# The state-space loop of a two-layer trunk: its order on four engines, its outer products, its rotation table and its rings of loads

## The chip, the core and the metric

The kernel runs on one core of a Trainium2 chip. The metric is the time of one launch on the device in microseconds, median of the runs shown. Engines: PE (TensorE), DVE (VectorE), ACT (ScalarE), POOL (GpSimd), and SP, which here only issues DMAs.

## The reference

Two residual layers over 512 tokens of width 1024: a state-space mixer (S5), then forgetting attention, each followed by a gated feed-forward block with a short convolution. Every sub-layer is preceded by an RMSNorm whose shift, scale and gate come from a conditioning vector (adaLN). The change touches the first mixer alone:

```
u = h @ w_in
lb = exp(lam * exp(log_dt))                      # complex, 64 groups of 64 states
h[t] = lb * h[t-1] + bb @ u[t]                   # per group: 16 channels drive 64 states
y[t] = Re(c @ h[t]) + d * u[t]
y = gelu(y);  y = y * sigmoid(y @ w_glu);  out = y @ w_out
```

## The kernel before

Everything is fp32. Activations lie as 8 blocks of 128 channels by 512 tokens. A float32 matrix product whose result must be exact is made from rounded parts (`w_hi`, `w_lo`: ACT rounds, DVE takes the rest) as three products; the first mixer's projection and its inner products run in plain fp32.

**The mixer.** Time is cut into B = 64 blocks of L = 8 tokens. Each of the KT = 8 steps m of the loop takes 8 groups (128 channels):

- *projection*: u of block m, eight products of `s5_w_in` with the normalized x (`a_x`, L1196). ACT evicts it (`uf`, L1198), SP writes it to DRAM (`s_ud`, L1201) and reads it back in another layout (`u`, L1203).
- *inputs* (`s5_inputs`): outer products of powers of lambda with B on DVE (`x`, L983, L987); PE multiplies them with `both` (planes of C and of an identity, filled by ACT, L995) into `aux` (L999); ACT evicts `w1` and the convolution kernel `kt` (L1004, L1008). `kt` plus the skip (`dd`, L1009) goes to DRAM (`s_z`) and comes back as a Toeplitz matrix (`tw`, L1016), which ACT masks (`t`, L1021).
- *scan* (`s5_scan`): PE makes the block sums (L1036), DVE rotates them by a table (`s_rot`), so that the recurrence over the 64 blocks becomes real, scans (L1058) and rotates back (`ua`, L1047 to L1068). `cf` are the scan's factors, made by ACT (L1053).
- *outer products out* (`s5_states_out`, `w2`, L963, L972) on DVE, and *outputs* (`s5_outputs`): the Toeplitz part (L1078), then the states' part (L1086), then gelu on ACT (`yg`, L1092) and a way through DRAM (`s_yd`) into `y`, L1096.

Between these, `ada_pe` computes the modulation vectors: each PE pair of products (L212) eats two tiles `raw` of 512 KB from `in_ada_w`. The first two thirds (scale, shift) stand in the startup, the gate and two thirds of the next sub-layer in the loop: twelve pairs, called modulation pairs here. Loads take rooms in rings: `raw` has three, `w_hi` and `w_lo` five each; a load waits until the room's last reader is done. The argument `n` of `raw()` chooses the ring.

**The startup** (up to the first L1196) computes the state-space parameters in small DVE operations of 128x32 (`s5_params`), interleaved with the root of the RMSNorm (`inv_root`, `rs_y`). The scale's columns give `ga` (L174), x is normalized (`a_x`, L1150), and the products of block 0 run between the loads of the shift; the shift is added afterwards by ACT (L1174, L1185) and, for block 0, through a product with the shift column (L1177).

**Order.** The startup stands in a `manual_schedule`: PE, ACT, DVE and SP issue what the program says, in its order. The loop was left to the framework's scheduler, which orders the instructions of all engines by its own cost model and the given priorities; `behind(...)` and `issue_after` only keep some of them from moving ahead. Behind the loop, the first four blocks of the glu product (`glu_head`, L1223) are interleaved the same way: part 0 with the rounded weights `hi`, made by ACT (L1257), part 1 with `lo`.

## Time and profile before

| | us |
|---|---|
| median of 3 runs | 1211.58 (1208.62 to 1212.55) |
| profiled execution, its own time | 1210.89 |
| its span | 1209.1 |
| startup, to the first projection in the loop | 43.0 |
| the loop's first to last block sums (L1036) | 64.7 to 162.9 |
| first product behind the mixer's gate head (L301, mmp) | 198.5 |

A row of a view by windows reads: stretch in us, then for each engine its busy time and the number of its instructions, the clock granted to PE (1.00 is full), the share of the DMA engines and GB/s. A row of a timeline: start, duration of the run of equal instructions, engine, line, operation, out<-in, shape, count, and in brackets the idle time ahead of it with what ended it. One matrix product in fp32 is two PE instructions in the trace. PEld are the weight loads, which overlap PE. SPq rows are the issues of DMAs, and the last number in a row of issues is the median from issue to landing.

### The profile page before, as it was taken

The page shows a single profiled execution, that of the slowest core. Times are in us where ns is not written, and L with a number is a line of the kernel's source. Part 1 is how long each engine was busy: PE and PEld are TensorE (multiplying, and loading weights), DVE is VectorE, ACT ScalarE, POOL GpSimd, SP SyncE. Part 2 cuts the span into 40 slices and gives each one's busy share as a digit, 9 for nine tenths or more (in the row PEclk, how much of TensorE's full clock was granted, in tenths as well). Part 3 has the DMA queues.
Part 4 walks back from the last instruction along what each step waited for, and adds up shares of the span by engine and source line. Part 5 has one row for each costly group of instructions (what it writes and reads, how often), then busy time and mean ns, then how long its engine had stood idle before and what let it go on. Part 6 is the DMA issues. An engine that isn't in the chain of part 4 may idle for free.

```text
span 1209.1 us, 20651 instructions
## 1 busy us (share of the span) xinstructions
PE 1179.1 (98%) x7925; PEld 1015.0 (84%) x7925; DVE 1010.3 (84%) x1900; ACT 612.4 (51%) x1172; POOL 91.1 (8%) x149
## 2 busy tenths in 40 slices
PE   7999999999999999999999999999999999999997
PEld 2566678898989889999899888878989999999987
DVE  7889986879889999998697578876899887888865
ACT  3564554336444455555443566664366555545543
POOL 0000001100000000000000344430000000000000
PEclk9999999999999999999999999999999999999999
DMA  8777787721455545433445543432223432323331
GB/s 334 242 251 247 225 292 272 256 98 36 131 159 172 171 156 165 159 107 97 127 145 193 168 160 126 150 117 94 76 65 102 122 119 82 114 93 110 110 100 70
DMA packets 72849, 181.73 MB, mean 150 GB/s; under 512 B 23103, under 2 KB 25503, under 8 KB 71727
## 3 DMA queue, kind: packets, MB, share of 16 engines
q1 hardware_dynamic: 66127, 156.82, 39.6%
q0 software_dynamic: 6336, 23.07, 5.8%
q8 instruction: 62, 1.02, 0.4%
q10 hardware_dynamic: 288, 0.52, 0.1%
q14 instruction: 36, 0.29, 0.1%
HBM read 173.47 MB, written 6.92 MB: 149 GB/s over the span
## 4 chain that ended last, share of the span: by engine, by line
PE 51%; issue 19%; DVE 17%; DMA 8%; ACT 2%; POOL 1%; SPq 0%; DVEq 0%; POOLq 0%; ACTq 0%
PE mmp L301 23%; PE mmp L570 10%; DVE w_lo L285 5%; PE aux L570 4%; PE mmp L1196 3%; PE mmp L1401 2%; PE aux L1540 2%; DVE conv L622 2%; PE aux L1560 1%; DVE sums L538 1%; DVE nm_t L538 1%; DVE ada_raw L254 1%; DVE h L383 1%; DMA rawd<-in_w_down 1%; PE aux L999 1%
## 5 line engine op out<-in xcount | busy, mean ns | idle before, releaser
L285 DVE TENSOR_TENSOR w_lo<-raw,w_hi 128x1024 fp32r<-128x1024 f32 (+4 forms) x173 | 184.9, 1074 | 25.2 <-ACT w_hi L284 24.7
L284 ACT ACTIVATE w_hi<-raw 128x1024 fp32r<-128x1024 f32 (+4 forms) x173 | 153.9, 899 | 100.6 <-PE mmp L301 47.2
L301 PE MATMUL mmp<-ghi,w_lo 128*128 128x512 f32 (+1 forms) x412 | 147.5, 358 | 1.2 <-DVE w_lo L285 1.2
L301 PE MATMUL mmp<-ghi,w_hi 128*128 128x512 f32 (+1 forms) x412 | 147.8, 359 | 0.3 <-DVE h L383 0.3
L301 PE MATMUL mmp<-glo,w_hi 128*128 128x512 f32 (+1 forms) x412 | 147.3, 358 | 0.0
L301 PE MATMUL mmp<-a_hi,w_hi 128*128 128x512 f32 (+1 forms) x344 | 126.0, 369 | 1.5 <-ACT a_hi L453 1.5
L301 PE MATMUL mmp<-a_hi,w_lo 128*128 128x512 f32 (+1 forms) x344 | 123.7, 360 | 0.0
L301 PE MATMUL mmp<-a_lo,w_hi 128*128 128x512 f32 (+1 forms) x344 | 123.4, 359 | 0.0
L570 PE MATMUL mmp<-w_hi 128*128 128x256 f32 x420 | 116.2, 277 | 1.5 <-DVE nm_t L538 1.3
L570 PE MATMUL mmp<-w_lo,w_hi 128*128 128x256 f32 x420 | 115.9, 276 | 0.0
L570 PE MATMUL mmp<-w_hi,w_lo 128*128 128x256 f32 x420 | 115.7, 276 | 0.0
L577 ACT ACTIVATE nm_h<-mmp 128x256 f32<-128x256 f32 x105 | 39.7, 381 | 108.8 <-PE mmp L570 108.8
L285 DVE TENSOR_TENSOR w_lo<-sums,w_hi 128x1024 fp32r<-128x1024 f32 x78 | 94.8, 1217 | 0.0
L284 ACT ACTIVATE w_hi<-sums 128x1024 fp32r<-128x1024 f32 x78 | 80.9, 1053 | 17.8 <-DVE sums L538 16.1
L301 PEld LDWEIGHTS mmp<-ghi,w_lo 128*128 128x128 f32 x412 | 77.4, 188 | 13.8 <-DVE w_lo L285 2.2
L301 PEld LDWEIGHTS mmp<-ghi,w_hi 128*128 128x128 f32 x412 | 77.4, 188 | 11.0 <-issue 0.5
L301 PEld LDWEIGHTS mmp<-glo,w_hi 128*128 128x128 f32 x412 | 77.4, 188 | 10.2
L570 PEld LDWEIGHTS mmp<-w_hi 128*128 128x128 f32 x420 | 78.8, 188 | 2.1 <-ACT w_hi L284 1.6
L383 DVE SCALAR_TENSOR_TENSOR h<-mmp,par,h 128x512 f32<-128x512 f32 (+1 forms) x104 | 68.6, 663 | 14.1 <-PE mmp L301 13.9
L570 PE MATMUL mmp<-a_hi,w_hi 128*128 128x256 f32 x280 | 78.0, 279 | 2.1 <-ACT nm_h L577 1.9
L570 PEld LDWEIGHTS mmp<-w_lo,w_hi 128*128 128x128 f32 x420 | 78.8, 188 | 0.0
L570 PE MATMUL mmp<-a_hi,w_lo 128*128 128x256 f32 x280 | 77.6, 277 | 1.2 <-DVE w_lo L285 1.2
(320 smaller groups left out, 3086.6 us busy)
## 6 DMA issues: line engine op xcount, KB each, us to landing
raw<-in_w_up SPq DMA_DIRECT2D x88, 512.0 KB, 3.3
raw<-in_ada_w SPq DMA_DIRECT2D x40, 512.0 KB, 5.0
ada_raw<-in_ada_t POOLq DMA_DIRECT2D x40, 512.0 KB, 4.5
nf<-nfd SPq DMA_DIRECT2D x8, 1152.0 KB, 7.1
raw<-in_fox_qk SPq DMA_DIRECT2D x16, 512.0 KB, 3.8
raw<-in_w_down SPq DMA_DIRECT2D x24, 320.0 KB, 2.9
rawd<-in_w_down SPq DMA_DIRECT2D x24, 256.0 KB, 3.3
raw<-in_w_down SPq DMA_DIRECT2D x16, 384.0 KB, 3.4
```

Source lines behind the costliest of these rows:

```text
L254: nc.vector.tensor_tensor_reduce(w, w, self.c_row, 1.0, 0.0, ALU.mult, ALU.add, sums[:, j:j + 1])
L284: self.rounded = nc.scalar.activation(hi, src, AF.Copy).ins
L285: return nc.vector.tensor_tensor(lo, src, hi.bitcast(F32), ALU.subtract)
L301: self.last_mm = self.nc.tensor.matmul(o if len(xt.shape) == 2 else by_place(o), wt, xt, start=(k == 0 and n == 0), stop=(k == nk - 1 and ...
L383: add = self.nc.vector.scalar_tensor_tensor(h, ps, self.par[i][:, 16 + m:17 + m], h, op0=ALU.mult, op1=ALU.add,)
L538: sub = lambda o, u, v, op=ALU.subtract: nc.vector.tensor_tensor(o, u, v, op)
L570: self.last_mm = nc.tensor.matmul(o, wt[:, k], xt[:, k], start=(first and k == 0 and n == 0), stop=(k == H - 1 and n == 2), skip_group_che ...
L577: a = nc.scalar.activation(t, o, AF.Copy)
L622: c = nc.vector.scalar_tensor_tensor(t[:, d:], ps[:, :S - d], cw[:, 2 - d, f:f + 1], t[:, d:], op0=ALU.mult, op1=ALU.add)
L1196: nc.tensor.matmul(ps, w[m][:, k, :], x[:, k], start=(k == 0), stop=(k == KT - 1))
L1401: self.last_mm = nc.tensor.matmul(ps[q, b][:, :n], xt[:, k, tb], wt, start=(k == 0 and i == 0), stop=(k == KT - 1 and i == 2),)
L1540: nc.tensor.transpose(pt[:, r - rs[0], k, :], s[:, r, k * P:(k + 1) * P], self.ident)
```

## The change

The loop and its prologue now stand in a `manual_schedule` too: the order on PE, ACT, DVE and SP is the program's. Within a step: block sums m, gelu of m-1, inputs of m+1, scan m, kernel of m+1, mask m, projection and outer products of m+2, outer products out of m+1, outputs of m, modulation pairs, factors and rotations. The pieces of `s5_inputs` are functions of their own.

The outer products for `w2` become two of 128x1024 instead of four of 128x512 (C lies as three planes side by side, one of them twice). The full rotation table goes: `s_rot` keeps the first 8 blocks, and two tiles `rot` of 8 pairs each are filled from it in turn, with a third plane for minus the sine, so that a rotated sum needs no split. `ada_pe` can load one pair ahead, and its loads and those of `s5_w_in` go round three rings instead of two (`n % 3`). In the startup the turns are interleaved with the parameters' last part, and the root stands behind both; some parameter work moves later.

```diff
             [(t, k) for t in thirds] for k in range(KT)
         ]
         n = 0
-        for step in steps:
+        ws = []
+
+        def load(step):
+            nonlocal n
+            for t, k in step:
+                ws.append(self.raw([P, D], self.io["ada_w"][i, k * P:(k + 1) * P, t * D:(t + 1) * D], n % 3))
+                n += 1
+
+        if ahead:
+            load(steps[0])
+            yield True
+        for s, step in enumerate(steps):
+            if not ahead:
+                load(step)
+            elif s + 1 < len(steps):
+                load(steps[s + 1])
             for j, (t, k) in enumerate(step):
-                w = self.raw([P, D], self.io["ada_w"][i, k * P:(k + 1) * P, t * D:(t + 1) * D], n % 2)
-                n += 1
+                w = ws.pop(0)
                 for q in range(2):
                     qq = 2 * j + q
...
-        y = self.inv_root(stats, NB, log=logs[0])
-        self.s5_turns(pool, co, si, logs[1])
-        in_turn(*logs)
-        yield y
+        self.s5_turns(pool, co, si, logs[0])
+        e = Ew(nc, tp, P, H, "e", ring=ring(0), log=logs[1])
...
-        nc.vector.reciprocal(rd, den)
+        e.do(lambda: nc.vector.reciprocal(rd, den))
         num = e.ts(br, -1.0, ALU.add)
         kr = e.add(e.mul(num, lre), e.mul(bi, lim))
         kr = e.mul(kr, rd, keep("kr"))
         ki = e.sub(e.mul(bi, lre), e.mul(num, lim))
         ki = e.mul(ki, rd, keep("ki"))
-        yield
+        in_turn(*logs)
+        yield self.inv_root(stats, NB)
         w1 = tp.tile([P, L, H], F32, name="s5_w1")
         w2 = tp.tile([P, L, H], F32, name="s5_w2")
 
...
+    def s5_rotations(self, m):
+
+        pairs = slice(m * 4, m * 4 + 8)
+        T = self.s5r.tile([P, 3, 8, B], F32, name="rot", bufs=2)
+        self.nc.scalar.activation(T[:, :2, :, :8], self.rot[:, :, pairs], AF.Copy)
+        self.s5_tables(T[:, :2], pairs, 3, 5)
+        yield
+        self.s5_tables(T[:, :2], pairs, 5, 6)
+        self.nc.scalar.activation(T[:, 2], T[:, 1], AF.Copy, scale=-1.0)
+        yield T
+
+    def s5_outer(self, m, l, b, a, tag):
+
         qs = slice(m * (GM // 2), (m + 1) * (GM // 2))
+        sh = [P, GM // 2, 2 * CG, L]
+        o = self.s5q.tile([P, GM // 2, 2, CG, L], F32, name=tag, bufs=1 if tag == "x" else 2)
+        self.nc.vector.tensor_tensor(
+            o.rearrange("p k r c j -> p k (r c) j"), l[:, qs, None, :].to_broadcast(sh),
+            b[:, qs, a:a + 2, :].rearrange("p k r c -> p k (r c)")[:, :, :, None].to_broadcast(sh), ALU.mult,
+        )
+        return o
+
+    def s5_sums(self, m, l, k, b, a, c, tag):
+
+        t1 = self.s5_outer(m, l, b, a, tag)
+        t2 = self.s5_outer(m, k, b, c, "x2")
         self.nc.vector.tensor_tensor(t1, t1, t2, ALU.add)
         return t1
 
+    def s5_states_out(self, m):
+        return self.s5_sums(m, self.er, self.ei, self.rr, 0, 1, "w2")
+
+    def s5_states_in(self, m):
+        return self.s5_sums(m, self.lr, self.li, self.bb, 1, 0, "x")
...
+    def s5_kernel(self, m, kt, dd):
+
+        nc = self.nc
         nc.vector.tensor_tensor(
             kt.rearrange("p c g -> p (c g)"), kt.rearrange("p c g -> p (c g)"), dd, ALU.add,
         )
+        nc.sync.dma_start(self.z[m][:P], kt.rearrange("p c g -> p (c g)"))
+
+    def s5_toeplitz(self, m):
+
         z = self.z[m]
         R = CG * GM
         tw = self.wpool.tile([P, L, CG, GM], F32, name="tw", tag="w_lo", bufs=WB)
...
+        turns = turns.rearrange("p r g b -> p r (g b)")
+        cb = turns[:, 0:1].to_broadcast([P, 2, W])
         v = ps.rearrange("p r g b -> p r (g b)")
         m1 = pool.tile([P, 2, W], F32, name="m1")
         m2 = pool.tile([P, 2, W], F32, name="m2")
         nc.vector.tensor_tensor(m1, v, cb, ALU.mult)
-        nc.vector.tensor_tensor(m2, v, sb, ALU.mult)
-        nc.vector.tensor_tensor(m1[:, 0], m1[:, 0], m2[:, 1], ALU.add)
-        nc.vector.tensor_tensor(m1[:, 1], m1[:, 1], m2[:, 0], ALU.subtract)
-        cf = pool.tile([P, 2, H4, B], F32, name="cf")
-        for k in range(H4):
-            nc.scalar.activation(
-                cf[:, :, k, :], self.mask[:, None, :].to_broadcast([P, 2, B]), AF.Copy,
-                scale=self.mag8[:, m * H4 + k:m * H4 + k + 1],
-            )
+        nc.vector.tensor_tensor(m2, v[:, ::-1], turns[:, 1:3], ALU.mult)
+        nc.vector.tensor_tensor(m1, m1, m2, ALU.add)
...
-                    w[m] = self.raw([P, KT, P], self.io["s5_w_in"][m], m % 2)
-
-                self.rot = keep.tile([P, 2, G // 2, B], F32, name="s5_rot")
+                    w[m] = self.raw([P, KT, P], self.io["s5_w_in"][m], m % 3)
+
+                self.rot = keep.tile([P, 2, G // 2, 8], F32, name="s5_rot")
...
-            ada = [self.ada_pe(i, (2,), late=True), self.ada_pe(i + 1, (0, 1), late=True)]
-            with self.behind(*behind):
-                for m in range(2):
-                    inputs(m)
-                ws[0] = self.s5_inputs(0)
-            for m in range(KT):
-                if m:
-                    outputs(m - 1)
-                if m > 1:
-                    self.s5_read_y(m - 2)
-                with self.behind(*behind):
-                    if m % 2 == 0:
-                        self.s5_tables(slice(m * 4, m * 4 + 8), 3, 6)
+            ada = itertools.chain(
+                self.ada_pe(i, (2,), late=True, ahead=True), self.ada_pe(i + 1, (0, 1), late=True, ahead=True)
+            )
+            with tc.manual_schedule(engines={ENG.PE, ENG.Activation, ENG.DVE, ENG.SP}):
+                ps = self.aux.tile([KT, P], F32, name="aux")
+                nc.tensor.transpose(ps, self.sc, self.ident)
+                rows = self.tmp.tile([KT, P], F32, name="nm_h", bufs=4)
+                self.s5_signs_c()
+                self.s5_planes_of(0)
+                for k in range(2, 4):
+                    nc.scalar.activation(x[:, k], x[:, k], AF.Identity, bias=self.par[i][:, k:k + 1])
+                load_d(0)
+                load_d(1)
+                load_w(2)
+                next(ada)
+                inputs(0)
+                for k in range(4, KT):
+                    nc.scalar.activation(x[:, k], x[:, k], AF.Identity, bias=self.par[i][:, k:k + 1])
+                read_u(0)
+                turns = self.s5_rotations(0)
+                next(turns)
+                self.s5_kernel(0, kts.pop(0), dds.pop(0))
+                rot = next(turns)
+                x_in[1] = self.s5_states_in(1)
+                w2s[0] = self.s5_states_out(0)
+                tws[0] = self.s5_toeplitz(0)
+                project(1)
+                read_u(1)
+                nc.scalar.activation(rows, ps, AF.Copy)
+                nc.sync.dma_start(self.scd, rows)
+                cfs[0] = self.s5_factors(0)
+                for m in range(KT):
+                    if m + 3 < KT:
+                        load_w(m + 3)
+                    if m + 2 < KT:
+                        load_d(m + 2)
+                    ps = self.s5_blocks(ws[m], us[m])
+                    if m:
+                        self.s5_gelu(m - 1, yps.pop(m - 1))
                     if m + 1 < KT:
-                        ws[m + 1] = self.s5_inputs(m + 1)
+                        self.s5_planes_of(m + 1)
+                        inputs(m + 1)
+                    st = self.s5_scan(rot[:, :, m % 2 * 4:m % 2 * 4 + 4], ps, cfs.pop(m))
+                    if m + 1 < KT:
+                        self.s5_kernel(m + 1, kts.pop(m + 1), dds.pop(m + 1))
+                    t = self.s5_masked(tws.pop(m))
+                    if m:
+                        self.s5_read_y(m - 1)
+                    if m + 1 < KT:
+                        tws[m + 1] = self.s5_toeplitz(m + 1)
                     if m + 2 < KT:
-                        inputs(m + 2)
-                    for _ in range((2, 2, 1, 1, 1, 1, 2, 2)[m]):
-                        next(ada[m >= 2])
-                    if m == 1:
-                        next(ada[0])
+                        project(m + 2)
+                        read_u(m + 2)
+                        x_in[m + 2] = self.s5_states_in(m + 2)
+                    if m == KT - 2:
+                        yhi = self.act.tile([P, KT, S], F32R, name="a_hi")
+                        ylo = self.act.tile([P, KT, S], F32R, name="a_lo")
+                    if m >= KT - 2:
+                        for n in (2 * m - 12, 2 * m - 11):
+                            raw[n] = self.raw([P, KT, P], self.io["s5_w_glu"][n], 2 * (n == HEAD - 1))
+                    if m + 1 < KT:
+                        w2s[m + 1] = self.s5_states_out(m + 1)
+                    yps[m] = self.s5_outputs(us.pop(m), t, w2s.pop(m), st)
+                    ws.pop(m)
+                    for _ in range((2, 2, 2, 2, 2, 1, 2, 1)[m]):
+                        next(ada)
+                    if m + 1 < KT:
+                        cfs[m + 1] = self.s5_factors(m + 1)
+                        if m % 2 == 0:
+                            if m + 2 < KT:
+                                turns = self.s5_rotations(m + 2)
+                                next(turns)
+                        else:
+                            rot = next(turns)
+                    if m == KT - 2:
+                        for k in range(4):
+                            parts(k)
                     if m == KT - 1:
+                        for k in range(4, 6):
+                            parts(k)
                         for n in range(HEAD):
-                            raw[n] = self.raw([P, KT, P], self.io["s5_w_glu"][n], 2 * (n == HEAD - 1))
                             hi[n] = part_of(self.wpool, [P, KT, P], "w_hi", "w_hi", WB)
                             nc.scalar.activation(hi[n], raw[n], AF.Copy)
                             gps[n] = self.mm.tile([P, S], F32, name="mmp")
-                    sts[m] = self.s5_scan(m, ws[m][0], us[m])
-                    with tc.issue_after(self.x_made):
-                        w2s[m] = self.s5_states_out(m)
-                if m == KT - 2:
-                    yhi = self.act.tile([P, KT, S], F32R, name="a_hi")
-                    ylo = self.act.tile([P, KT, S], F32R, name="a_lo")
-                    for k in range(m - 2):
-                        parts(k)
-                if m >= KT - 2:
-                    parts(m - 2)
-            outputs(KT - 1)
-            for m in range(KT - 2, KT):
-                self.s5_read_y(m)
+                self.s5_gelu(KT - 1, yps.pop(KT - 1))
+                for m in range(KT - 2, KT):
+                    self.s5_read_y(m)
             for k in range(KT - 1):
                 if k == KT - 2:
                     parts(k)
```

Three places in the order. First SP's queue in step 3 of the loop. The names are the destinations and sources of DMAs: `s_ud`, `u` for the way of u, `s_z`, `tw` for the Toeplitz matrix, `s_yd`, `h` for the way of y, `raw<-in_ada_w` a modulation tile; brackets name the semaphores waited for (DMAHW: a landing). Before, in a step of the middle:

```order
L1093 DMA s_yd<-yg 128x8x64 [waits DMAHW5_49,Activation_49]
L1016 DMA tw<-s_z 128x1024 [waits DMAHW6_49,DMAHW2_49]
L1201 DMA s_ud<-uf 128x512 [waits DMAHW7_49,Activation_49]
L1096 DMA h<-s_yd 128x512 [waits DMAHW5_49,DMAHW0_49]
L193 DMA raw<-in_ada_w 128x1024 [waits DMAHW1_49,PE_49]
L1203 DMA u<-s_ud 128x8x64 [waits DMAHW7_49]
L193 DMA raw<-in_ada_w 128x1024 [waits DMAHW3_49]
```

Now, in step 3:

```order
L1143 DMA s_yd<-yg 128x8x64 [waits DMAHW7_49,Activation_49]
L1043 DMA s_z<-kt 128x128 [waits DMAHW0_49,DVE_49]
L1146 DMA h<-s_yd 128x512 [waits DMAHW7_49]
L1050 DMA tw<-s_z 128x1024 [waits DMAHW2_49,DMAHW0_49]
L1248 DMA s_ud<-uf 128x512 [waits DMAHW3_49,Activation_49]
L1252 DMA u<-s_ud 128x8x64 [waits DMAHW4_49,DMAHW3_49,PE_49]
L193 DMA raw<-in_ada_w 128x1024 [waits DMAHW5_49]
L193 DMA raw<-in_ada_w 128x1024 [waits DMAHW6_49]
L193 DMA raw<-in_ada_w 128x1024 x2
```

The four modulation tiles of a step (two for its own second pair, two for the first pair of the next) now stand behind the write of u and its read, one after the other.

Second, PE in a step of the middle, from one block sum to the next. Before:

```order
L1036 MATMUL aux<-u,w_1065 64x64 x16
L1078 MATMUL aux<-u,t 128x64 x8
L999 MATMUL aux<-s_both_137,x 128x2x80 x2
L1196 MATMUL mmp<-a_x,raw 128x512
L999 MATMUL aux<-s_both_137,x 128x2x80 x2
L1196 MATMUL mmp<-a_x,raw 128x512
L999 MATMUL aux<-s_both_137,x 128x2x80 x4
L1196 MATMUL mmp<-a_x,raw 128x512 x4
L1086 MATMUL aux<-ua,w_1316 128x63 x16
```

Now, step 4:

```order
L1083 MATMUL aux<-u,w_1096 64x64 x16
L1025 MATMUL aux<-s_both_138,x 128x2x80 x8
L1245 MATMUL mmp<-a_x,raw 128x512 x8
L1122 MATMUL aux<-u,t 128x64 x8
L1130 MATMUL aux<-ua,w_1162 128x63 x16
L226 MATMUL mmp<-raw,s_sc_206 32x512 x8
```

The projection, which stood in pieces between the inputs, is one run, and the two modulation pairs (x8) close the step instead of standing between projection and block sums.

Third, ACT at the loop's end. `ada_rows` is the eviction of the modulation sums, `a_hi` a rounded part of y, `w_hi` a rounded weight of the glu head, `yg` a gelu. Before:

```order
L1257 ACTIVATE w_hi<-raw 128x1024
L219 ACTIVATE ada_rows<-mmp 128x512
L1053 ACTIVATE cf<-s_mask,s_mag_181 128x2x64
L1021 ACTIVATE t<-tw,first 128x16x8 x8
L1053 ACTIVATE cf<-s_mask,s_mag_181 128x2x64 x3
L1257 ACTIVATE w_hi<-raw 128x1024
L1092 ACTIVATE yg<-aux 128x256 x2
```

Now:

```order
L298 ACTIVATE a_hi<-h 128x512 x4
L1142 ACTIVATE yg<-aux 128x256 x2
L1059 ACTIVATE t<-tw,first 128x16x8 x8
L233 ACTIVATE ada_rows<-mmp 128x512
L298 ACTIVATE a_hi<-h 128x512 x2
L1362 ACTIVATE w_hi<-raw 128x1024 x4
```

The roundings of the glu head's weights, of which the first stood ahead of the last mask, are now one run behind the eviction of the last modulation pair.

More of the change, by code (lines that the diff above doesn't have):

```diff
@@ L194, in raw, with ada_pe @@
         return t
-    def ada_pe(self, i, thirds, late=False):
+    def ada_pe(self, i, thirds, late=False, ahead=False):
         nc = self.nc
@@ L853, in s5_params @@
         keep = lambda n: tp.tile([P, H], F32, name=f"s5_{n}")
-        ring = lambda n: tp.tile([P, (24, 36, 24)[n], H], F32, name=f"s5_ring{n}")
+        ring = lambda n: (
+            tp.tile([P, 36, H], F32, name="s5_ring1") if n == 1 else
+            self.s5q.tile([P, 24, H], F32, name=f"s5_ring{n}", tag="t", bufs=3)
+        )
         e = Ew(nc, tp, P, H, "e", ring=ring(0))
@@ L952, in s5_tables @@
         return last.ins
-    def s5_outer(self, m, l1, b1, l2, b2, tags):
-        nc = self.nc
-        qs = slice(m * (GM // 2), (m + 1) * (GM // 2))
-        sh = [P, GM // 2, CG, L]
-        out = []
-        for l, b, tag in ((l1, b1, tags[0]), (l2, b2, tags[1])):
-            o = self.s5q.tile([P, 2, GM // 2, CG, L], F32, name=tag, bufs=1 if tag == "x" else 2)
-            for r in range(2):
-                nc.vector.tensor_tensor(
-                    o[:, r], l[:, qs, None, :].to_broadcast(sh), b[:, r, qs, :, None].to_broadcast(sh), ALU.mult
-                )
-            out.append(o)
-        return out
@@ L1287, in s5 @@
                 self.mms(gps[HEAD], more, (yhi, ylo), k, KT, slice(0, S))
[L1288 removed]
+            next(ada)
         self.h = self.y
```

139 lines of the change are left out of this document (70 added, 69 removed).

## The prediction, made before the changed kernel ran

> **What bounds the kernel now.** First the page's busy shares, then the view by windows over the stage that the change rewrites (0 to 198 us of the trace), since an average over the program says nothing about a stage.
>
> ```profile
> PE 1179.1 (98%) x7925; PEld 1015.0 (84%) x7925; DVE 1010.3 (84%) x1900; ACT 612.4 (51%) x1172; POOL 91.1 (8%) x149
> ...
> 0.00:43.00 43.00, 33.62 (x145) 13.61 (x146) 33.63 (x176) 12.91 (x23) 2.67 (x22) 1.00 0.84 315
> 43.00:162.00 119.00, 117.77 (x880) 73.11 (x880) 107.60 (x172) 63.94 (x203) 0.00 (x0) 0.99 0.75 236
> 162.00:175.00 13.00, 11.97 (x133) 10.28 (x132) 11.99 (x19) 8.72 (x21) 1.81 (x3) 1.00 1.00 342
> 175.00:198.00 23.00, 23.00 (x106) 19.08 (x104) 15.08 (x24) 7.90 (x11) 4.25 (x8) 1.00 0.84 281
> ```
>
> From 43 us on PE is the bound: it idles 1.23 us of 119, then 1.03 of 13, then nothing. So whatever the change saves on DVE or ACT there is worth 2.3 us at the most, and every wait that the new order gives to PE is paid in full. Only before 43 us has PE 9.4 us to gain. Behind the stage PE's instructions stand in the same order as before, and PE is busy there; I take the difference at 198 us as the difference of the whole.
>
> One step of the loop, from PE's timeline:
>
> ```profile
> 57.18 2.34 PE L999 MATMUL aux<-s_both,x 128*128 128x160 f32 x16
> ...
> 130.10 1.15 PE L1036 MATMUL aux<-u,w 128*64 128x64 f32 x32
> 131.18 2.00 PE L1078 MATMUL aux<-u,t 128*128 128x64 f32 x16
> ...
> 136.96 3.60 PE L1196 MATMUL mmp<-a_x,raw 128*128 128x512 f32 x8
> 140.52 2.00 PE L1086 MATMUL aux<-ua,w 64*128 64x63 f32 x32
> ...
> 144.36 1.06 PE L212 MATMUL mmp<-raw,s_sc 128*32 128x512 f32 x8
> 145.36 0.86 PE L1036 MATMUL aux<-u,w 128*64 128x64 f32 x22
> ```
>
> By start to start: blocks 1.08, inputs 2.2, projection 6.9 (twice the x8 row less its overlap), outputs 1.93 and 1.93, one modulation pair 1.0: 15.0 of the 15.26 us between the two blocks (130.10 to 145.36). The scheduler fills a wait for DVE with pieces of a projection or of the modulation.
>
> **Startup.** The rows for the loads, the two things that x waits for, and the last modulation load:
>
> ```profile
> raw<-in_ada_w SPq DMA_DIRECT2D x40, 512.0 KB, 5.0
> ...
> 3.70 5.18 SPq L193 DMA_DIRECT2D raw<-in_ada_w  x6
> 17.49 1.75 SPq L193 DMA_DIRECT2D raw<-in_ada_w  x4
> ...
> 10.00:15.00 5.00, 5.00 (x12) 1.49 (x10) 4.61 (x38) 2.77 (x5) 0.00 (x0) 1.00 1.03 419
> 15.00:20.00 5.00, 3.49 (x29) 1.20 (x28) 3.50 (x38) 0.60 (x1) 0.00 (x0) 1.00 0.66 226
> ...
> 14.65 0.19 DVE L928 SCALAR_TENSOR_TENSOR s_turn<-s_si 128x32 f32<-128x32 f32 x1
> 16.50 0.16 DVE L411 TENSOR_SCALAR rs_v<-aux 128x4 f32<-128x4 f32 x1 [1.65 <-PE aux L1139]
> ...
> 19.52 0.15 DVE L421 TENSOR_TENSOR rs_y<-rs_y,rs_t 128x4 f32<-128x4 f32 x1
> 25.53 0.17 DVE L174 SCALAR_TENSOR_TENSOR ga<-aux,rest 128x8 f32<-128x8 f32 x1 [3.17 <-PE aux L169]
> 32.21 1.40 DVE L1150 SCALAR_TENSOR_TENSOR a_x<-h,ga,aux 128x512 f32<-128x512 f32 x2
> ...
> 29.91 6.89 DMA raw<-in_ada_w
> ...
> 41.09 1.95 PE L1177 MATMUL aux<-par,raw 128*128 128x1 f32 x16 [0.27 <-ACT par L177]
> ```
>
> SP sends six modulation tiles and then stands until 17.49, because the seventh needs a room of the ring of three; the rate falls from 419 to 226 GB/s. With three rings all eight go out. Ahead of the last tile the queue then has about 11.8 MB (16 tiles, two other weights, x, two packs); at 419 GB/s from 3 us that is 31.2 us, against 36.80. DVE allows it: of its small steps 35 now stand between 16.50 and 19.52, 0.09 us each, interleaved; then 42 run from 14.65 without the wait for the statistics, to some 18.6, and the eleven of the root behind them, alone and each waiting for the last, near 0.2 each: rs_y at 21 (now 19.52). The rows and columns on PE take 2.2 to 2.4 us more, so ga comes at 23.4 instead of 25.53, and the last a_x ends at 31.5 instead of 33.6. Both inputs of the shift's products move by about 5 us. **-5.4 us**; bounds: -2.3 (only the hole from 15 to 20, 0.97 MB) and -7.
>
> **The bridge to the loop.** What ACT and DVE do there:
>
> ```profile
> 43.01 8.73 PE L1196 MATMUL mmp<-a_x,raw 128*128 128x512 f32 x16
> ...
> 43.95 3.77 ACT L1185 ACTIVATE a_x<-a_x,par 128x512 f32<-128x512 f32 x6
> ...
> 42.66 1.22 DVE L983 TENSOR_TENSOR x<-s_lr,s_bb 128x1024 f32<-128x1024 f32 x1
> 43.80 1.22 DVE L983 TENSOR_TENSOR x<-s_li,s_bb 128x1024 f32<-128x1024 f32 x1
> ```
>
> Now PE goes straight into a projection. In the new order inputs(0) comes first and needs the planes, which ACT makes behind the shift, u, and the sign of C: about 2.3 us of idle PE. Then blocks(0) is done near 51 us, but the outer products of step 1 (three wide ones, 1.14 apart, 3.5 us) stand on DVE behind the rotations, and these behind ACT's six shifts of a_x (3.77) and eight evictions: they end near 54, another 2.9 us. Against it, the projection at 43 ran 1.5 us long (8.73 for two of 3.6), and that loss now falls into idle time. **+3.7 us**, bounds 1 and 6 (no wait for the planes; a late C).
>
> **The loop.** DVE gains: four outer products of 128x512 become two of 1024, the rotated sums lose a split. That is 0.3 us of a step in which DVE is not the bound:
>
> ```profile
> 116.07 0.69 DVE L1047 TENSOR_TENSOR m<-aux,s_rot 128x512 f32<-128x512 f32 x1
> ...
> 120.91 0.69 DVE L1068 TENSOR_TENSOR ua<-ua,ub 128x512 f32<-128x512 f32 x1
> ```
>
> The scan's chain takes 5.5 us now and about 5.3 then, its result is ready 6.4 us into a step, and PE wants it at 12.1: covered by inputs and projection (9.1 us), as long as there is a projection. The fixed order itself saves the 0.25 us a step of the interleaving, **-1.5 us**.
>
> The price is in SP's queue. In a step with two modulation pairs, the second pair's load stands behind the read of u, and that waits until u is written, which waits for ACT's eviction of the projection. Nothing else can pass.
>
> ```profile
> 129.88 0.32 SPq L1201 DMA_DIRECT2D s_ud<-uf  x1
> ...
> 131.91 0.37 SPq L1203 DMA_DIRECT2D u<-s_ud  x1
> 132.38 1.01 SPq L193 DMA_DIRECT2D raw<-in_ada_w  x2
> ...
> raw<-in_ada_w SPq DMA_DIRECT2D x4, 512.0 KB, 4.9
> tw<-s_z SPq DMA_DIRECT2D x2, 512.0 KB, 3.9
> s_ud<-uf SPq DMA_DIRECT2D x2, 256.0 KB, 2.1
> s_z<-kt SPq DMA_DIRECT2D x1, 64.0 KB, 1.5
> ...
> DMA to landing us min/median/max: 3.9/4.9/10.2
> ```
>
> From the projection's end: 0.75 to the issue of the write (eviction and queue), 2.1 to its landing, 0.47 to the next issue (131.91 to 132.38), 4.9 to the landing: 8.2 us. PE has outputs (3.86) and one pair (1.0): 4.9. It waits 3.4 us, in the steps 0, 1, 3 and 4 (step 2 multiplies no pair, step 5 has one, loaded a step ahead): **+13.4 us**. Bounds: a landing of 3.9 gives 9.4, one of 5.9 gives 17.4. What is queued behind the waiting product on PE is the next step's blocks, so DVE's scan moves by as much; DVE's own work, 107.60 us in 119 or 13.8 in a step of 15.26, leaves room in one of 18. Before, the scheduler had loads ahead, and other products stood between.
>
> **The tail.** Steps 6 and 7 have no projection to cover the scan. Step 6: blocks, inputs and half the outputs end 5.2 us in, the scan at 6.5: 1.3 us. Then the second pair: its load stands behind the Toeplitz read, which waits for the kernel's write (kernel sum at 6.7, landing 1.5 to 2.4), and behind two glu loads; issue near 10.2, landing 15.1, wanted at 9.4: 5.7 us. Step 7: 1.08 + 1.93 of work before the scan's 6.5: 3.4 us. Then the glu head, whose four roundings now stand on ACT behind the modulation rows of the last pair:
>
> ```profile
> 159.67 1.06 ACT L1257 ACTIVATE w_hi<-raw 128x1024 fp32r<-128x1024 f32 x1
> ```
>
> Rows and two parts of y take 1.8 us, the first rounding ends 2.8 us after the last pair, and the third weight's load waits for that pair's room (4.9 to land, then 1.0): 4.0 us idle. Less the 2.3 us of idle PE that the present order has: **+12.1 us**, bounds 7 and 16. y's second read of block 6 hides behind the glu products.
>
> Sum: -5.4 + 3.7 - 1.5 + 13.4 + 12.1 = **+22.3 us**. The profiled execution took 1210.89 (span 1209.1 and 1.8 around it), in line with the median of 1211.58: forecast **1233 us**. All low ends together give about 1219, all high ends 1247.
>
> **Half clock, the first rival.** After 3 us of tiny products PE ran at half clock:
>
> ```profile
> 44.00:46.00 2.00, 2.00 (x4) 0.74 (x3) 2.00 (x3) 2.00 (x5) 0.00 (x0) 0.50 0.70 164
> ```
>
> If each of the six long waits (3.3 us or more) is followed by such a stretch at 1.5 us, 9 us are added: **1242 us**. Against it: the row from 15 to 20 us has 1.5 us of idle PE and clock 1.00, so a wait must be longer than that to count. [...]
>
> **Softer waits, the second.** Landings near 3 us on a queue that is less loaded, and a quick glu load: 4 x 1.5 instead of 13.4, tail 7, startup -7: +8, **1219 us**. For it: DMA is busy 0.75 in the loop. Against: the least landing of a weight there is 3.9.
>
> **Faster, the third, on the other side.** The modulation pair is there when PE wants it, and with it the tail's. Then -5.4 + 3.7 - 1.5 - 2.3 remain: **1205 us**. It decides at a landing of 1.5 us (0.75 + 2.1 + 0.47 + 1.5 = 4.8); nothing in the trace lands that soon. That the startup gains far more, from PE's 9.4 us, leads to the same side. **No change, the fourth:** half of the waits, and 7 us at the start: 1211.
>
> **How the numbers follow.** Forecast (1222 to 1239) 0.56; half clock (1239 to 1247) 0.12; softer (1214.5 to 1222) 0.16; no change 0.07; faster 0.09. A change within 0.3% (3.6 us) is about what a measurement of this kernel can't tell from none. Faster by more than that 0.09, within 0.07, slower 0.84. The range takes the first three cases: 1214 to 1245.
>
> **What would show it.** Startup: eight modulation loads in one go, the shift's products (L1230 now) near 36 us. Loop: in PE's waits the modulation line (L226), released by its own load, four times about 3 us and once 5 or more; steps of 19 us with two pairs and of 15 without. Tail: PE idle before the outputs' second half in step 7, and before the first glu products, released by ACT. The forecast is wrong if the modulation tiles have landed when PE gets there, or if DVE's chain, not a load, releases PE in the middle steps.

## The result

The changed kernel took **1264.18 us** (median of 4 runs, 1262.48 to 1266.22), the kernel before 1210.1 on the same chip: a ratio of 1.0448, 95% interval 1.0418 to 1.0477. The direction was forecast, the size was not: +54 us against +22, outside the range. The profiled run of the changed kernel has a span of 1264.5 us, 55.4 more than before.

The page's busy shares after the change:

```profile
PE 1204.5 (95%) x7925; PEld 1033.7 (82%) x7925; DVE 1013.8 (80%) x1868; ACT 616.3 (49%) x1179; POOL 89.1 (7%) x149
```

PE has the same 7925 instructions as before and is busy 25.4 us longer. The view by windows over the stages says why: startup, bridge (to the first projection behind the second block of inputs), steps 0 to 5, tail. First the changed kernel, then the same stages before:

```profile
0.00:40.40 40.40, 33.23 (x145) 13.65 (x145) 35.82 (x175) 13.02 (x23) 2.67 (x22) 1.00 0.88 343
40.40:62.30 21.90, 17.15 (x82) 12.56 (x82) 13.08 (x22) 12.58 (x35) 0.00 (x0) 0.77 0.45 137
62.30:186.30 124.00, 105.09 (x708) 64.41 (x706) 84.27 (x110) 45.80 (x148) 0.00 (x0) 0.88 0.52 165
186.30:252.20 65.90, 54.61 (x334) 42.27 (x331) 41.77 (x58) 29.96 (x64) 6.74 (x12) 0.82 0.77 264
```

```profile
43.00:65.00 22.00, 22.00 (x90) 11.51 (x90) 19.07 (x28) 14.95 (x46) 0.00 (x0) 0.92 0.68 225
65.00:153.95 88.95, 87.72 (x698) 56.10 (x692) 82.40 (x136) 47.21 (x156) 0.00 (x0) 1.00 0.76 234
153.95:198.53 44.58, 43.55 (x341) 35.39 (x339) 33.73 (x53) 18.91 (x36) 6.06 (x11) 1.00 0.88 299
```

Length less PE's busy time is the **idle time**. The granted clock, for each half microsecond, gives a second term: busy time times (1 - clock) is what PE lost by running at half speed (0.50 in the clock's column): the states' part of the outputs (L1130) took 3.68 us at 0.50 in step 6 and 2.00 at 1.00 in step 0. Summed over windows of 0.5 us:

| | idle, before | idle, after | lost to half clock, before | after |
|---|---|---|---|---|
| bridge | 0.0 | 4.8 | 1.7 | 4.5 |
| steps 0 to 5 | 1.2 | 18.9 | 0.0 | 11.8 |
| tail | 1.0 | 11.3 | 0.0 | 10.5 |

The startup ends 2.6 us earlier (40.4 against 43.0). So -2.6 + 32.7 of idle time + 25.1 of half clock = 55.2 us; the first product behind the mixer's gate head comes 53.7 later (252.2 against 198.5), so that 1.5 us of work were saved besides. Behind it another 1.7 us arise, with PE's work and order as before: they are one more stretch at half clock (481.80 to 485.21 us), and why it came is not shown. Nearly half of the loss is the clock.

The waits of PE in the changed kernel, by what ended them (total, number, longest; the row with `nm_t` is the startup's):

```profile
PE mmp L226 <- DMA raw<-in_ada_w: 15.9, 6, 4.7
PE mmp L1184 <- ACT nm_t L1183: 5.9, 1, 5.9
PE aux L1025 <- ACT s_both L1012: 4.5, 3, 1.6
PE aux L1130 <- DVE ua L1112: 3.5, 1, 3.5
PE aux L1122 <- ACT t L1059: 3.2, 1, 3.2
PE mmp L1276 <- ACT w_hi L1362: 2.7, 1, 2.7
PE aux L1025 <- DVE x L997: 2.5, 1, 2.5
PE aux L1025 <- issue: 2.2, 1, 2.2
```

The modulation tiles lead, as forecast. Step 0 on PE's timeline, from the projection to the next:

```profile
62.28 7.03 PE L1245 MATMUL mmp<-a_x,raw 128*128 128x512 f32 x16
69.15 1.89 PE L1122 MATMUL aux<-u,t 128*128 128x64 f32 x16
70.97 2.00 PE L1130 MATMUL aux<-ua,w 64*128 64x63 f32 x32
72.91 1.07 PE L226 MATMUL mmp<-raw,s_sc 128*32 128x512 f32 x8
78.65 3.20 PE L226 MATMUL mmp<-raw,s_sc 128*32 128x512 f32 x8 [4.67 <-DMA raw<-in_ada_w]
81.78 1.44 PE L1083 MATMUL aux<-u,w 128*64 128x64 f32 x32
```

and SP's timeline at the same place: u is written 0.7 us behind the projection's end, read 3.0 later, and only then do the tiles go out, to land 5.2 us after their issue:

```profile
69.97 0.32 SPq L1248 DMA_DIRECT2D s_ud<-uf  x1
73.00 0.37 SPq L1252 DMA_DIRECT2D u<-s_ud  x1
73.42 2.00 SPq L193 DMA_DIRECT2D raw<-in_ada_w  x4
```

The second pair itself takes 3.20 us instead of 1.07. Windows of 1 us around that wait (first PE's busy time, third number from the end the clock):

```profile
73.00:74.00 1.00, 0.97 (x8) 0.06 (x8) 0.97 (x2) 0.98 (x4) 0.00 (x0) 1.00 0.00 0
...
75.00:76.00 1.00, 0.00 (x0) 0.00 (x0) 0.93 (x4) 0.00 (x0) 0.00 (x0) 0.81 1.04 255
76.00:77.00 1.00, 0.00 (x0) 0.00 (x0) 0.30 (x1) 0.00 (x0) 0.00 (x0) 0.50 0.89 324
...
81.00:82.00 1.00, 1.00 (x6) 0.23 (x6) 0.00 (x0) 0.00 (x0) 0.00 (x0) 0.50 0.96 365
82.00:83.00 1.00, 1.00 (x32) 1.00 (x30) 0.00 (x0) 0.00 (x0) 0.00 (x0) 0.78 1.03 344
```

Of the windows of 0.5 us from 40 to 252 us all but seventeen, those with an edge in them, read 1.00 or 0.50. So a window with 0.81 is at half clock for 0.38 of its length, one with 0.78 for 0.44: the clock fell at 75.62 and rose at 82.44, 6.82 us later, of which PE worked 3.8. Worked out in the same way there are nine such stretches between 40 and 226 us, of 6.8, 3.4, 6.8, 6.8, 6.8, 6.8, 3.4, 10.2 and 13.7 us: one to four times 3.41. The falls stand 17.1, 17.1, 23.9, 23.9, 20.5, 23.9, 27.3 and 17.1 us apart, all multiples of 3.41 too. In this trace the edges of the clock thus lie on one grid of 3.41 us, and a fall cost whole pieces of it, 1.7 us for each that PE worked through.

### The profile page after: what moved, and what is told of

The parts are those of the page before. It is cut to its first block, busy times and chain, and to the rows that moved or that the text cites. A ratio compares the mean times of both kernels' runs of the same rounds, so it can differ in the third digit from the quotient of the medians.

```text
span 1264.5 us, 20610 instructions
## 1 busy us (share of the span) xinstructions
PE 1204.5 (95%) x7925; PEld 1033.7 (82%) x7925; DVE 1013.8 (80%) x1868; ACT 616.3 (49%) x1179; POOL 89.1 (7%) x149
## 5 line engine op out<-in xcount | busy, mean ns | idle before, releaser
L299 DVE TENSOR_TENSOR w_lo<-raw,w_hi 128x1024 fp32r<-128x1024 f32 (+4 forms) x173 | 185.7, 1079 | 28.6 <-ACT w_hi L298 25.2
L584 PEld LDWEIGHTS mmp<-w_hi,w_lo 128*128 128x128 f32 x420 | 78.7, 188 | 0.1
```

The source lines that it names most:

```text
L299: return nc.vector.tensor_tensor(lo, src, hi.bitcast(F32), ALU.subtract)
L584: self.last_mm = nc.tensor.matmul(o, wt[:, k], xt[:, k], start=(first and k == 0 and n == 0), stop=(k == H - 1 and n == 2), skip_group_che ...
```

## The experiments

The theory, A in the expectations: the order in the queues makes PE wait, and the waits make the half clock. Its rivals: B, other things are as late as the tiles; C, the half clock has another cause. Times are medians; ratios are against the kernel before in the same comparison, with 95% intervals (changed kernel: 1.0448).

**Two pairs ahead** (and once more on the chip of the last comparison):

```diff
             load(steps[0])
+            load(steps[1])
...
-            elif s + 1 < len(steps):
-                load(steps[s + 1])
+            elif s + 2 < len(steps):
+                load(steps[s + 2])
```

> The changed kernel with every modulation pair loaded two pairs ahead instead of one, so that what SP sends behind the read of u is for the next step and not for this one. Changed kernel: 1264.2 us; before: 1210.1. Theory A (the queue makes the waits, the waits make the half clock): the four waits for the modulation tiles (4.7, 3.8, 3.3 and 4.0 us) go, and with them the half-clock stretches behind them (2.1 to 2.9 us each, about 10); 15.8 + 10 less what shows up behind them: steps 1 and 4 then get the wait for the planes (1.4 to 1.6 us) that steps 2, 3 and 6 have now. About 1242 us, between 1236 and 1248. Theory B (the scan or u is as late as the tiles): the waits move to the states' part of the outputs or to the block sums, and it stays above 1255. Theory C (the half clock has another cause than the waits): only the waits go, 1248.

1236.75 us, 1.0232 (1.0186 to 1.0277). PE's waits of this kernel:

```profile
PE aux L1026 <- ACT s_both L1013: 5.4, 3, 2.4
PE aux L1131 <- DVE ua L1113: 3.5, 1, 3.5
...
PE mmp L227 <- DMA raw<-in_ada_w: 0.4, 2, 0.2
```

The tiles' 15.9 us are 0.4. The order in SP's queue made these waits, and by the medians they cost 24 to 27 us with all that hung on them (by the repeat below and by this run). In the traces the first product behind the mixer's gate head comes 22.7 us earlier (229.5 against 252.2); 13.5 us of that are idle time and 5.3 half clock, of which 21.5 us are still lost. So only half of the expected 10 us of half clock went: longer waits in the bridge and for the planes (2.4 us) brought stretches of their own. Theory B falls; the planes became 0.9 us later, as expected of the next in line, though not in two more steps.

**Filled waits**: twelve products with a zero weight tile, then four.

```diff
+            for _ in range(self.fill if ahead else 0):
+                nc.tensor.matmul(
+                    ps[0:32, :], self.nil, self.fill_x, start=False, stop=False, tile_position=(0, 0),
+                    skip_group_check=True,
+                )
             for j, (t, k) in enumerate(step):
```

> The changed kernel with twelve products of a zero weight tile (128x32, 512 columns, 0.27 us each at full clock, 3.2 us together) ahead of the second modulation pair in steps 0, 1, 3 and 4; they add zero to the modulation sums. Loads and waits are as in the changed kernel, but PE works in them. Theory A (idle time of PE makes the half clock): the tiles land when they did, the idle time of these four waits goes from 15.8 to about 3 us while the end of the wait stays where it is, and the clock holds 1.00 behind them: 10 us less, 1254. Theory C (the half clock follows from the kind of work or from the clock's own rhythm): the stretches stay, 1262 to 1266. If such narrow products do not count as work for the clock, also 1264.

1279.17 us, 1.0576 (1.0545 to 1.0607), a miss: the fill took 10.0 us and not 3.2, at 0.87 us a product (the 0.27 expected is a quarter of the 1.07 us that the modulation's four take together). So it ran with four:

> As the kernel with twelve zero products in each of the four waits, but with four. The twelve took 10.0 us, 0.87 each, since one 32-column product stands alone where the modulation's four run side by side; that outlasted the waits by some 5 us each and so made the kernel longer, though the clock read 1.00 behind them. Four take 3.5 us, about a wait. Theory A (idle PE makes the half clock): the wait ends when it did, nothing is at half clock behind it, 2.1 to 2.9 us less at each of the four: 1254, between 1250 and 1258. Theory C: the stretches come anyway, 1264 or a little above.

1262.52 us, 1.0428 (1.0393 to 1.0463). Windows over the four filled waits and what follows each:

```profile
73.00:85.00 12.00, 10.58 (x87) 5.26 (x84) 6.11 (x12) 2.92 (x11) 0.00 (x0) 1.00 0.84 266
95.00:106.00 11.00, 8.19 (x68) 2.80 (x66) 3.66 (x7) 3.07 (x10) 0.00 (x0) 1.00 0.53 174
140.00:150.00 10.00, 8.96 (x77) 3.94 (x74) 1.11 (x3) 1.77 (x6) 0.00 (x0) 1.00 0.92 299
160.00:172.00 12.00, 11.51 (x103) 6.17 (x103) 5.42 (x11) 2.59 (x11) 0.00 (x0) 1.00 0.79 244
```

The clock holds 1.00 in all four: at these places idle PE was the cause, Theory C falls. But the time fell by 1.7 us, not by 10, which can't be told from nothing. The pair ended only 0.7 to 1.0 us sooner at each place, since its tiles land one by one and hold PE anyway: in this run one tile's products took 1.05 us by themselves, as long as the products of two tiles that are both there (1.06). And in step 2 the wait for the planes grew from 1.5 to 2.4 us and brought its own stretch. Where the next thing was late too, what the clock lost was partly covered: the changed kernel lost 8.9 us there, and the medians differ by 1.7.

**Planes a step early:**

```diff
-                        self.s5_planes_of(m + 1)
...
+                    if m + 2 < KT:
+                        self.s5_planes_of(m + 2)
                     if m + 1 < KT:
                         cfs[m + 1] = self.s5_factors(m + 1)
```

> The changed kernel with the planes of C for a step made one step earlier on ACT, ahead of the factors, instead of behind the gelu of the step. Theory A: the three waits of the inputs for the planes (1.5, 1.6 and 1.4 us, 4.5 together) go, and the half-clock stretch that follows the one in step 3 (5.7 us at half clock, 2.9 lost) goes or moves: 1257, between 1255 and 1261. Rival (ACT is late as a whole): the wait moves to the next thing that PE wants of ACT, the evictions of the inputs or the masks, and it stays at 1263 or above.

1261.78 us, 1.0439 (1.0408 to 1.0470): no difference. The wait for the planes was replaced by

```profile
PE aux L1025 <- DVE m L1100: 1.8, 1, 1.8
PE aux L1025 <- ACT yg L1142: 1.4, 2, 0.7
```

that is, for a room in the ring of four that the inputs, block sums and outputs share: the gelu and the scan's first operations had not read the old tiles. The time lies between the two expectations; the wait moved, as the rival had it, though to other operations than it named.

**Two rings in the startup:**

```diff
-t * D:(t + 1) * D], n % 3))
+t * D:(t + 1) * D], n % (3 if ahead else 2)))
```

> The changed kernel with the startup's modulation loads (scale and shift) back on two rings instead of three; the loop's stay on three. If the third ring is what brought the startup forward, the last tile of the shift lands some 2 us later, the products with the shift's column start near 41 instead of 38.4, and the time is 1266 to 1267. If the order of the startup did it, the column's products stay near 38.4 and the time at 1264.

1265.58 us, 1.0469 (1.0431 to 1.0506). The column's products start at 41.89, not 38.42: the third ring is the startup's gain, 3.5 us. The time can't be told from the changed kernel's. In the trace this kernel idled 3.0 us longer behind its startup than the changed one, but lost only 20.9 us to half clock instead of 26.8: its waits fell otherwise on the grid of 3.41 us, on which its edges lie too (80.43 and 87.26, 111.15 and 114.57, 172.59 and 176.01, 199.90 and 206.73, 213.55 and 227.21), and this makes up for most of the 3.0 and the startup's 3.5 us.

**Four outer products** instead of two wide ones:

```diff
-        self.nc.vector.tensor_tensor(
-            o.rearrange("p k r c j -> p k (r c) j"), ...
+        for h in (slice(0, GM // 4), slice(GM // 4, GM // 2)):
+            self.nc.vector.tensor_tensor(
+                oq[:, h], lq[:, h, None, :].to_broadcast(sh), bq[:, h, :, None].to_broadcast(sh), ALU.mult,
+            )
```

> The changed kernel with each wide outer product split again into two of half the groups (128x512), as the kernel before had them for the outputs; inputs too. That is 0.07 to 0.15 us more DVE work for each of 32 products. If DVE's saving is worth nothing where the loads hold PE: 1264, within 3 us. If DVE's chain sets the length of a step: 0.3 to 0.6 us a step, 1267 to 1269.

1264.69 us, 1.0445 (1.0407 to 1.0484): the wide products are worth nothing here. The two small rotation tables and the third ring of the loop's loads were not run apart; what they cost or gain alone is not shown.

**Another order with the same parts:**

```diff
+                    t = self.s5_masked(tws.pop(m))
+                    st = self.s5_scan(rot[:, :, m % 2 * 4:m % 2 * 4 + 4], ps, cfs.pop(m))
+                    if m + 2 < KT:
+                        project(m + 2)
+                        read_u(m + 2)
...
+                        inputs(m + 1)
+                        w2s[m + 1] = self.s5_states_out(m + 1)
...
+                    yps[m] = self.s5_outputs(us.pop(m), t, w2s.pop(m), st)
+                    self.s5_gelu(m, yps.pop(m))
```

> The changed kernel's parts (wide outer products, small rotation table, three rings) with another fixed order: pairs loaded two ahead; in a step block sums, projection, inputs, outputs, so that the projection covers the scan, the planes and the gelu; ACT's masks first in a step, gelu right behind the outputs, planes a step early; in the startup the planes of block 0 ahead of the shift's columns, in the bridge the outer products of block 1 ahead of the rotations; in steps 6 and 7 the modulation pairs between block sums and outputs, glu loads and roundings earlier. Theory A (the loss is this order's waits and the half clock they bring, nothing in the parts): PE idles less than 8 us between the shift's column products at 38.4 and the first product behind the glu head, which then comes near 200 us, and the time is 1207, between 1200 and 1216. Rival (a fixed order with these parts cannot keep PE busy, because DVE or the loads are late whatever the order): waits of 2 us or more a step remain, above 1225.

1223.68 us, 1.0109 (1.0067 to 1.0152). Between the two theories: steps 1 to 4 run without a wait, here step 1 on PE,

```profile
71.73 1.15 PE L1084 MATMUL aux<-u,w 128*64 128x64 f32 x32
72.81 7.13 PE L1248 MATMUL mmp<-a_x,raw 128*128 128x512 f32 x16
79.78 2.34 PE L1026 MATMUL aux<-s_both,x 128*128 128x160 f32 x16
81.96 1.89 PE L1123 MATMUL aux<-u,t 128*128 128x64 f32 x16
83.78 2.00 PE L1131 MATMUL aux<-ua,w 64*128 64x63 f32 x32
85.71 1.92 PE L227 MATMUL mmp<-raw,s_sc 128*32 128x512 f32 x16
87.57 1.15 PE L1084 MATMUL aux<-u,w 128*64 128x64 f32 x32
```

15.84 us with both pairs, against 22.3 in the changed kernel's step 1. What stays is 3.9 us for u of block 0, read behind five loads of 512 KB, 3.0 and 4.6 for the masks of steps 6 and 7 (the first ends, by its row, with an eviction that ACT makes right behind the mask), and their half clock. The next two kernels took these on, one wait after the other:

```diff
+                    if KT - 4 < m < KT - 1:
+                        inputs(m + 1)
                     st = self.s5_scan(rot[:, :, m % 2 * 4:m % 2 * 4 + 4], ps, cfs.pop(m))
+                    if KT - 4 < m < KT - 1:
+                        self.s5_kernel(m + 1, kts.pop(m + 1), dds.pop(m + 1))
+                        tws[m + 1] = self.s5_toeplitz(m + 1)
```

> The reordered kernel with its four remaining stalls mended: u of block 0 read ahead of the modulation and projection loads (PE waited 3.9 us for it), in steps 5 and 6 the inputs ahead of the projection and the way of the Toeplitz matrix ahead of the modulation and glu loads (waits of 3.0 and 4.6 us), the modulation's column products between projection and inputs in step 2 (their 1.4 us of tiny products brought a half-clock stretch). Theory A: of the reordered kernel's 12.0 us of idle PE and 13.3 us lost to half clock behind the startup 3 to 6 us in all remain; the time is 1203, between 1197 and 1210, below the kernel before. Rival (the waits move on, to the scan of step 7, the glu loads, the way of u): 1213 or more.

1222.24 us, 1.0104 (1.0076 to 1.0132). The waits moved: 4.3 us for the outer products of block 7 on DVE, 2.6 for a projection weight, 3.6 for modulation tiles. In the last kernel of this line a projection weight and three glu weights load earlier and sixteen glu products stand ahead of the last Toeplitz part:

```diff
+                    if m == KT - 3:
+                        x_in[m + 2] = self.s5_states_in(m + 2)
...
+                        for n in (0, 1, 3, 2):
+                            for k in range(2):
+                                for xt in (yhi, ylo):
...
+                        t = self.s5_masked(tws.pop(m))
```

> The mended kernel with its remaining waits taken on: the projection weight of block 2 loaded in the startup (wait of 2.6 us), in step 5 the outer products of block 7 ahead of those for the outputs (4.3), the last modulation pair and three glu weights loaded a step earlier (1.1 and 1.8), and in step 7 sixteen glu products between modulation and Toeplitz part, with the glu weights' roundings on ACT ahead of the last mask. Theory A (every wait of a fixed order is one of its own places and can be covered): of 12.2 us idle and 12.5 us lost to half clock behind the startup no more than 3 and 4 stay; 1206, between 1200 and 1212. Rival (in the tail there is too little PE work beside scan, masks and loads, whatever the order): 4 us or more of waits stay behind step 5 and bring half clock, 1214 or above.

1223.39 us, 1.0107 (1.0083 to 1.0131). The rival held twice. PE's longest wait behind the startup is now 3.4 us, for the planes of block 7. Behind it SP's timeline shows another holder:

```profile
160.65 2.03 SPq L193 DMA_DIRECT2D raw<-in_ada_w  x4
162.78 1.63 SPq L193 DMA_DIRECT2D raw<-in_s_w_glu  x3
...
165.76 0.33 SPq L1047 DMA_DIRECT2D s_z<-kt  x1
174.03 0.32 SPq L1054 DMA_DIRECT2D tw<-s_z  x1
```

The read, which waits for the write of 64 KB, was issued 8.3 us behind it, and seven loads of 512 KB had been issued in the 5.1 us ahead of the write; in the changed kernel such a write landed 1.5 us after its issue (median of seven). The fourth glu weight stood behind that read in SP's queue (174.45), and PE then waited 2.5 us for ACT, which had waited for this weight. So loads sent early enough to be no wait of their own stood here ahead of a small transfer that the next step hangs on, and it came late; that the loads held it is argued from the order and the two times, not shown by a run of its own. Whether a fixed order with these parts can beat the kernel before stays open; three tries ended at 1.01.

**Filled tail**: the kernel with two pairs ahead, with three zero products in each of three waits of the tail.

```diff
+        if fill == 2:
+            self.fill_in(self.ada_ps)
         for k in range(H4):
             for r in range(2):
```

> The kernel with pairs loaded two ahead, with three zero products (2.6 us at full clock) in each of its three long waits of the tail: for the masks in step 6 (3.2 us), for the scan in step 7 (3.5), for the first rounded glu weight (2.7). They add zero to sums or are overwritten. In that kernel 10.6 us of the tail's 67 are lost to half clock. Theory A' (half clock is caused by idle PE, and where no load or other engine is late behind it, all of it is paid): the tail's waits end where they did, the clock stays at 1.00, 7 to 10 us less than the same kernel without them in the same comparison (1236.8 there): 1228. Rival (as with the filled waits for the tiles, where 10 us lost to half clock were worth only 1.7: what follows is late anyway): 1234 or more.

> The kernel with pairs loaded two ahead once more, so that the kernel with the filled tail is compared with it on one chip: 1237, between 1233 and 1241.

1235.38 us, 1.0225 (1.0201 to 1.0249), with the fill, and 1239.98 us, 1.0248 (1.0225 to 1.0270), without. The tail by windows, with the fill and then without (up to about the same product):

```profile
165.00:220.00 55.00, 50.41 (x309) 35.77 (x310) 40.08 (x55) 27.23 (x60) 6.75 (x12) 1.00 0.88 295
```

```profile
165.00:228.00 63.00, 52.16 (x308) 40.75 (x303) 40.60 (x57) 29.04 (x63) 6.78 (x12) 0.81 0.77 254
```

The clock is full and the first product behind the tail comes at 220.8 instead of 229.1, 1.3 of which the filled kernel was ahead at the tail's start: 7.0 us gained of 10.6 lost there. A wait of 2.2 us for a part of y (`a_lo`), which the kernel without the fill does not have, takes most of the rest. The whole executions differ by 4.6, with intervals that overlap.

**The third ring alone, in the kernel before:**

```diff
-[i, k * P:(k + 1) * P, t * D:(t + 1) * D], n % 2)
+[i, k * P:(k + 1) * P, t * D:(t + 1) * D], n % (3 if thirds in ((0,), (1,)) else 2))
```

> The kernel before with one thing of the change: the startup's modulation loads (scale and shift) go round three rings; everything else is the scheduler's as before. In the changed kernel the third ring alone moved the shift's column products by 3.5 us (38.4 against 41.9). If the startup's gain is the loads', and PE stays busy behind it: 2 to 3.5 us less than before, 1207. If PE then waits in the loop for what the startup no longer hides, or the scheduler's changed order costs as much: 1210 or more.

1206.26 us, 0.9966 (0.9951 to 0.9982): a third of a per cent below the kernel before, and the fastest of all these kernels.

```profile
37.16 1.95 PE L1177 MATMUL aux<-par,raw 128*128 128x1 f32 x16 [0.27 <-ACT par L177]
...
39.08 8.73 PE L1196 MATMUL mmp<-a_x,raw 128*128 128x512 f32 x16
```

The loop starts 3.9 us earlier and PE stays busy behind it. This is the part of the change that is a gain.

## Why the prediction was wrong

**The step that failed is the half clock.** The prediction had it as a rival, with 0.12, at 9 us: six waits at 1.5 us each, and none below 3.3. The price came from the one stretch of the trace of before (0.50 in 44 to 46 us, 8.73 us for 7.2), as a possible extra to waits that were taken as near certain. Measured are nine stretches, 26.8 us against 1.7 before.

The length of a wait alone, in the prediction anything over 1.5 us, does not decide. In the piece of 3.41 us ahead of each fall PE was idle for 0.6 to 3.4 us; the 0.6 are in step 3, where the clock fell at 123.40, that long into a wait of 1.61, behind products of 2 and 8 columns. The waits of 1.52 and 1.42 us brought no fall: they left 1.2 us and less in any one piece, beside the inputs' products. A stretch ended, all nine times, at the end of a piece with 0.6 us of idle time at the most, but pieces filled with the outputs' products of 63 and 64 columns (195 to 202 us) did not end theirs; the nine took one to four pieces, and 3.0 us of work were lost on the mean.

Of those nine pieces two were idle nearly throughout (3.4 and 3.3 us), the other seven for only 0.6 to 2.9. By the measured 1.7 us, an estimate, six waits at one to two pieces, 1.7 to 3.4 us each, would have made the forecast 1243 to 1253. Where the four waits for the tiles or the three of the tail were filled, the clock held 1.00. What it cost net was less than its 25 us where another load or engine was late behind it: 1.7 of the 8.9 that the four stretches behind the tiles took, 7.0 of 10.6 in the tail.

**Startup, forecast -5.4, measured -2.6.** Right in mechanism: the loads go round three rings at

```profile
15.00:20.00 5.00, 4.31 (x32) 1.28 (x32) 4.83 (x44) 0.60 (x1) 0.00 (x0) 1.00 1.01 392
```

where the rate had been 226; the root ends at 21.04 (forecast 21), the last `a_x` at 31.59 (31.5), `ga` at 24.0 (23.4). The size was off: the shift's last tile landed at 34.2, not 31.2, so that the column's products stood at 38.42. The estimate had 11.8 MB at 419 GB/s from 3 us on; measured are 12.4 MB at 396 GB/s until 34.2, so that the rate and the uncounted bytes make about half of the 3.0 us each. That the uncounted bytes are those of C and a projection weight, issued right behind the tile, is argued, not shown. In the kernel before with the third ring alone, where B's 512 KB are issued behind the last tile and not ahead of it, the column's products stand at 37.16; at 396 GB/s 512 KB take 1.3 us, as much as the difference.

**Bridge, +3.7.** Its two waits were forecast at 2.3 and 2.9 and came at 2.2 and 2.5. The 1.5 us that should have been absorbed were not: half clock cost 4.5 there, 2.8 more than before.

**Fixed order, -1.5, and DVE's savings, nothing.** The table of the result leaves 1.5 us of work saved, but that is a remainder and its agreement with the forecast is luck: it has in it some 2.5 us (an estimate from the four pairs of L226 that wait: 13.3 us, 6.5 of them lost to half clock, against 4.3) by which tiles that land one by one make a pair longer. The direct evidence is step 5, the one with a single pair and no wait: 15.0 us (171.35 to 186.33) against 15.26. The run with four outer products bears out the second.

**Modulation pairs, +13.4.** Measured 15.8 in steps 0, 1, 3 and 4 (4.7, 3.8, 3.3, 4.0), by the mechanism and at the places forecast; the run with two pairs ahead showed it. Unforeseen were the planes, 4.5 us in steps 2, 3 and 6: ACT makes them behind the gelu, which stands behind factors and rotations. The prediction had followed ACT's queue in bridge and tail only.

**Tail, +12.1.** Measured 10.3 more idle time, but spread otherwise. Step 7's scan: 3.50, forecast 3.4. Glu head: 2.7 and 0.5, forecast 4.0. In step 6 the scan hides behind ACT's masks, which come behind eight evictions (3.2), and the load that was to cost 5.7 had landed when PE, by then late, got there.

Without the clock the terms measure 28.6 us (-2.6 + 32.7 - 1.5) against 22.3, between their joint ends of 9 and 36; the clock nearly doubled them. The rival on the other side (tiles there when wanted) did not happen; what it would have left, a startup that is worth 3 to 5 us, is what the third ring shows.

## What to carry to other kernels

A wait given to a PE that was always busy was priced twice here: by its length, and at nine places by the half-clock pieces behind it, 1.7 us each and one to four of them; both belong in the sum, not among the rivals. In a hand order, look in each queue for transfers that stand behind a wait they don't need, above all bulk loads behind a round trip through DRAM (waits of 3.3 to 4.7 us here), and then for small transfers that stand behind bulk loads (8.3 us, once). And take a change of many parts apart: one argument, `n % 3` in the startup's loads, was worth 3.5 us by itself, and all parts together cost 54.

## What the hardware showed that was not expected

Clock: it fell once without any idle time. In the reordered kernel PE shows no wait between 101 and 105 us, yet behind 1.3 us of products with 2 and 8 columns the clock goes to 0.61 and 0.50:

```profile
102.00:103.00 1.00, 1.00 (x16) 0.98 (x17) 1.00 (x2) 0.96 (x5) 0.00 (x0) 1.00 0.12 33
103.00:104.00 1.00, 1.00 (x30) 1.00 (x28) 0.97 (x2) 0.06 (x1) 0.00 (x0) 0.61 0.62 74
104.00:105.00 1.00, 1.00 (x9) 0.69 (x6) 1.00 (x2) 0.00 (x0) 0.00 (x0) 0.50 1.02 225
```

The piece of 3.41 us ahead of this fall (at 103.22) held only those and products of 63 and 64 columns. In the next two kernels the same tiny products stand right behind a projection, and no stretch followed them. The reverse holds too: pieces of the reordered kernel that were idle for 1.7 us beside products of 512 columns (48.61 to 52.02 and 168.07 to 171.49) brought no fall. So in these traces the idle time of a piece does not settle whether the clock falls; that the kind of work in it counts as well is a guess from these few pieces, not shown by a run.

Products of 512 columns with a zero weight tile of 32 columns, on the other hand, held it at 1.00 (72.0 to 110.6 us with twelve in each wait, and the four windows with four). Such a product took 0.87 us alone, while the modulation's four, which the kernel puts at four positions of 32 columns, took 1.07 together.
